# Binary cross-entropy on one core: the last full store moved to GpSimd's DMA queue, and two sets of fourteen tiny SBUF copies on SyncE

## The chip, the core and the metric

The kernel runs on one core of a Trainium2 chip. The metric is device time in microseconds of one execution; a median of several runs is given. The engines that matter are VectorE (DVE), ScalarE (ACT), GpSimd (POOL) and SyncE (SP). The first three compute or issue transfers here; SP only issues transfers. All transfers, whoever issues them, are carried out by the core's 16 DMA engines.

## The reference

```python
def setup_inputs():
    return {
        "pred": np.random.uniform(0.01, 0.99, (8192, 8192)).astype(np.float32),
        "target": np.random.randint(0, 2, (8192, 8192)).astype(np.float32),
    }

def reference(pred, target):
    eps = 1e-7
    pred = np.clip(pred, eps, 1 - eps)
    return -(target * np.log(pred) + (1 - target) * np.log(1 - pred))
```

Every element is independent. Two inputs of 256 MB each are read, one output of 256 MB is written. Targets are 0 or 1, so the loss is -log|target - 1 + pred|, and that is how the kernel computes it.

## The kernel before

The flat arrays are cut into 39 chunks, each seen as 128 partitions by some width. Chunk 0 has 8192 columns, chunks 1 to 35 have 14336 each (`WIDE`), and three tail chunks have 6656, 6656 and 1024 (`TAIL`). The index of the last wide chunk, 35, is called `z`; the tail chunks are called `a`, `b` and `c`. Prediction chunks live in a ring of three slots (`ring_p`, fp32); chunk z has the third slot, and a, b, c share the first. Target chunks live in one slot (`ring_t`), which the load converts to bf16; a, b and c take disjoint columns of it.

For each chunk there are six steps. `load_p` and `load_t` (lines 70 and 73) bring the data in. `clip` (DVE, line 85) clips the prediction in place. `merge` computes target - 1 + pred on DVE (line 91), then the absolute value and the logarithm on ACT (lines 94 and 95). `negate` (DVE, line 99) changes the sign. `store` (line 79) writes the result out. Wide chunks are computed in two halves of their columns, tail chunks in one piece.

The schedule is written by hand: each engine does its instructions in the order in which the program names them. Loads go through GpSimd's queue, apart from the first, which ACT issues. Stores go through GpSimd's queue too, up to chunk z - 1; the stores of z, a, b and c go through SP's. The last store, of chunk c, is split by rows into 108, 12 and 8 (`ROWS`).

In the loop over chunks k, the program merges k, loads the target of k + 1, negates k, clips k + 1, stores k and loads the prediction of k + 2. After the loop, chunk z is merged, and the six loads of a, b and c are issued on GpSimd. Then the order on DVE is: negate the first half of z, clip a, negate the second half of z, merge a, clip b, merge b, negate a, clip c, merge c, negate b, negate c; each store is issued by its queue when the chunk's negate is done.

Of the kernel before, what the change touches and what calls it, by code (L numbers as in the profile page):

```python
# [1 line left out]

# [4 lines left out]

EPS = 1e-7

WIDE = 14336  # L10
SLOTS = 3
TAIL = (6656, 6656, 1024)
ROWS = (108, 12, 8)


@with_exitstack
def kernel(
    ctx: ExitStack,
    tc: tile.TileContext,
    pred: bass.AP,  # L20
    target: bass.AP,
    out: bass.AP,
):
    nc = tc.nc
    fp32 = mybir.dt.float32
    low = mybir.dt.bfloat16
    Alu = mybir.AluOpType
    Act = mybir.ActivationFunctionType
    P = nc.NUM_PARTITIONS

    R, C = pred.shape
    total = R * C // P
    rest = total - sum(TAIL)
    n = rest // WIDE
    first = rest - n * WIDE
    assert 0 < first <= WIDE and n > 4 and sum(TAIL) <= WIDE
    spots = [(first, 0)]
    spots += [(WIDE, k % SLOTS * WIDE) for k in range(1, n + 1)]
    c = (n + 1) % SLOTS * WIDE
    for w in TAIL:  # L40
        spots.append((w, c))
        c += w
    n = len(spots)
    z = n - 1 - len(TAIL)
    starts = [sum(w for w, _ in spots[:k]) * P for k in range(n)]

    pool = ctx.enter_context(tc.tile_pool(name="rings", bufs=1))
    ring_p = pool.tile([P, SLOTS * WIDE], fp32, name="ring_p", tag="ring_p")
    ring_t = pool.tile([P, WIDE], low, name="ring_t", tag="ring_t")
    warm = pool.tile([1, 8], fp32, name="warm", tag="warm")  # L50

    def chunk(ap, k):
        flat = ap.rearrange("r c -> (r c)")
        w = spots[k][0]
        return flat[starts[k] : starts[k] + w * P].rearrange("(p w) -> p w", p=P)

    def cols(ring, k, part, c):
        w = spots[k][0]
        i, m = part
        return ring[:, c + i * w // m : c + (i + 1) * w // m]  # L60

    def p_of(k, part=(0, 1)):
        return cols(ring_p, k, part, spots[k][1])

    def t_of(k, part=(0, 1)):
        return cols(ring_t, k, part, spots[k][1] % WIDE)

    def load_p(k):
        queue = nc.scalar if k == 0 else nc.gpsimd
        queue.dma_start(out=p_of(k), in_=chunk(pred, k))  # L70

    def load_t(k):
        nc.gpsimd.dma_start(out=t_of(k), in_=chunk(target, k))  # L73

    def store(k):
        queue = nc.sync if k >= z else nc.gpsimd
        r = 0
        for rows in ROWS if k == n - 1 else (P,):
            queue.dma_start(out=chunk(out, k)[r : r + rows, :], in_=p_of(k)[r : r + rows, :])  # L79
            r += rows  # L80
        assert r == P

    def clip(k, *part):
        p = p_of(k, *part)
        nc.vector.tensor_scalar(  # L85
            out=p, in0=p, scalar1=EPS, scalar2=1 - EPS, op0=Alu.max, op1=Alu.min
        )

    def merge(k, *part):
        p, t = p_of(k, *part), t_of(k, *part)  # L90
        nc.vector.scalar_tensor_tensor(  # L91
            out=p, in0=t, scalar=1.0, in1=p, op0=Alu.subtract, op1=Alu.add
        )
        nc.scalar.activation(out=p, in_=p, func=Act.Abs)  # L94
        nc.scalar.activation(out=p, in_=p, func=Act.Ln)  # L95

    def negate(k, *part):
        p = p_of(k, *part)
        nc.vector.tensor_scalar(out=p, in0=p, scalar1=-1.0, scalar2=None, op0=Alu.mult)  # L99

    halves = (0, 2), (1, 2)
    with tc.manual_schedule():
        load_p(0)
        load_t(0)
        load_p(1)
        nc.vector.memset(warm, 1.0)  # L106
        nc.scalar.activation(out=warm, in_=warm, func=Act.Ln)  # L107
        for h in halves:
            clip(0, h)
        for k in range(z):  # L110
            for h in halves:
                merge(k, h)
            load_t(k + 1)
            for h in halves:
                negate(k, h)
            for h in halves:
                clip(k + 1, h)
            store(k)
            if k + 2 <= z:
                load_p(k + 2)  # L120
        for h in halves:
            merge(z, h)
        a, b, c = range(z + 1, n)
        for j in a, b, c:
            load_p(j)
            load_t(j)
        negate(z, halves[0])
        clip(a)
        negate(z, halves[1])
        store(z)  # L130
        merge(a)
        clip(b)
        merge(b)
        negate(a)
        store(a)
        clip(c)
        merge(c)
        negate(b)
        store(b)
        negate(c)  # L140
        store(c)


# [1 line left out]
_INS = ['pred', 'target']  # L145
_OUTS = [((8192, 8192), 'float32')]


# [23 lines left out]
```

## Time and profile before

| what | value |
|---|---|
| median of 3 runs | 1882.25 us (1881.54 to 1882.39) |
| the profiled execution, its own time | 1880.78 us |
| its span, first to last instruction | 1879.0 us |
| DVE busy | 1118.3 us, 60% of the span |
| ACT busy | 901.7 us, 48% |
| POOL busy (issuing transfers) | 282.8 us, 15% |
| GpSimd's queue (q0) | 652.22 MB in 16128 packets |
| SP's queue (q1) | 14.68 MB in 592 packets |
| ACT's queue (q10) | 4.19 MB in 144 packets |

The span runs from the first to the last instruction of one execution under the profiler; it and the runs' times are close but not the same, so a sum made on the span has to be carried over to the runs. In the profile, "L79" is line 79 of the kernel, "SPq" and "POOLq" are the sequencers that issue transfers, and `out<-in` names what an instruction writes and reads. The rows of busy slices cut the span into 40 equal parts; a digit 9 means 90% busy or more. "GB/s" in these rows counts the bytes on the SBUF side, where a target element has two bytes after its conversion; the HBM line counts all four. A wait in square brackets is the time the engine stood idle just before an instruction, and what ended it.

### The profile page before, as it was taken

To read this page: it belongs to the slowest core of one execution; us is meant where nothing else is said; L and a number is where in the kernel's file an instruction comes from. 1 tells how busy PE (TensorE), PEld (TensorE's weight loads), DVE (VectorE), ACT (ScalarE), POOL (GpSimd) and SP (SyncE) were. 2 spreads that over 40 slices of the span, in tenths; PEclk is the share of its full clock that TensorE was granted. 3 is DMA by queue.
4 is the path that set the end of the run, shared out by engine and by line. 5 is a ranking of instruction groups with operands and counts; after the bars stand their busy time and mean duration, and the time that the engine had idled before them with its cause. 6 is when DMAs were issued, how large, how long until landed. Compare 5 with 4: busy or idle time off the path is not lost.

```text
span 1879.0 us, 697 instructions
## 1 busy us (share of the span) xinstructions
DVE 1118.3 (60%) x226; ACT 901.7 (48%) x152; POOL 282.8 (15%) x116
## 2 busy tenths in 40 slices
DVE  4675566565555665556656555566555666665563
ACT  3555444444455555554444444555555444444473
POOL 0121111111111110111111111111101111111100
DMA  9999999999999999999999999999999999999996
GB/s 329 338 375 372 370 352 366 355 352 352 359 359 355 355 371 376 374 373 359 359 358 358 352 353 361 358 354 364 375 374 374 369 353 363 355 354 354 359 363 239
DMA packets 16869, 671.14 MB, mean 357 GB/s; under 512 B 1888, under 2 KB 1888, under 8 KB 2272
## 3 DMA queue, kind: packets, MB, share of 16 engines
q0 software_dynamic: 16128, 652.22, 97.0%
q1 hardware_dynamic: 592, 14.68, 1.8%
q10 hardware_dynamic: 144, 4.19, 0.6%
q14 instruction: 5, 0.04, 0.0%
HBM read 536.87 MB, written 268.44 MB: 429 GB/s over the span
## 4 chain that ended last, share of the span: by engine, by line
DMA 64%; issue 28%; ACT 3%; DVE 2%; another core or an unknown queue 1%; POOL 0%; POOLq 0%; DVEq 0%; PEldq 0%
DMA ring_t<-in_target_dram 64%; ACT ring_p L95 2%; ACT ring_p L94 2%; DVE ring_p L91 2%; DVE ring_p L99 0%; POOL out_dram L79 0%; DVE ring_p L85 0%; POOL ring_p L70 0%; DVEq L167 0%; POOLq L73 0%; POOLq L79 0%; DVEq L91 0%; PEldq L167 0%
## 5 line engine op out<-in xcount | busy, mean ns | idle before, releaser
L94 ACT ACTIVATE ring_p<-ring_p 128x7168 f32<-128x7168 f32 (+3 forms) x75 | 451.6, 6021 | 959.1 <-DVE ring_p L91 959.1
L91 DVE SCALAR_TENSOR_TENSOR ring_p<-ring_t,ring_p 128x7168 f32<-128x7168 bf16 (+3 forms) x75 | 554.8, 7437 | 252.2 <-DMA ring_t<-in_target_dram 252.2
L99 DVE TENSOR_SCALAR ring_p<-ring_p 128x7168 f32<-128x7168 f32 (+3 forms) x75 | 285.0, 3802 | 475.0 <-ACT ring_p L95 475.0
L95 ACT ACTIVATE ring_p<-ring_p 128x7168 f32<-128x7168 f32 (+3 forms) x75 | 452.1, 6029 | 2.4
L85 DVE TENSOR_SCALAR ring_p<-ring_p 128x7168 f32<-128x7168 f32 (+3 forms) x75 | 281.9, 3799 | 20.3 <-DMA ring_p<-in_pred_dram 20.3
L79 POOL DMA_DIRECT2D out_dram<-ring_p x35 | 126.9, 3625 | 710.8 <-DVE ring_p L99 710.8
L73 POOL DMA_DIRECT2D ring_t<-in_target_dram x39 | 20.7, 532 | 801.1 <-DVE ring_p L91 800.3
L70 POOL DMA_DIRECT2D ring_p<-in_pred_dram x38 | 135.3, 3561 | 0.0
L107 ACT ACT_TABLE_LOAD x1 | 1.3, 1283 | 1.1 <-PEq L156 1.1
L106 DVE MEMSET warm<- 1x8 f32 x1 | 0.1, 65 | 0.8 <-PEq L156 0.8
L107 ACT ACTIVATE warm<-warm 1x8 f32<-1x8 f32 x1 | 0.2, 208 | 0.0
L156 POOL MEMSET const-float32-0.0<- 128x1 f32 x1 | 0.1, 100 | 0.2 <-issue 0.2
L156 POOL MEMSET const-bfloat16-1.0<- 128x1 bf16 x1 | 0.1, 102 | 0.0
L156 POOL MEMSET const-float32-1.0<- 128x1 f32 x1 | 0.1, 100 | 0.0
L156 POOL MEMSET const-uint8-127<- 128x1 uint8 x1 | 0.1, 99 | 0.0
## 6 DMA issues: line engine op xcount, KB each, us to landing
ring_p<-in_pred_dram POOLq DMA_DIRECT2D x35, 7168.0 KB, 44.4
out_dram<-ring_p POOLq DMA_DIRECT2D x34, 7168.0 KB, 31.0
ring_t<-in_target_dram POOLq DMA_DIRECT2D x35, 3584.0 KB, 35.2
out_dram<-ring_p SPq DMA_DIRECT2D x1, 7168.0 KB, 28.9
ring_p<-in_pred_dram POOLq DMA_DIRECT2D x2, 3328.0 KB, 34.7
out_dram<-ring_p SPq DMA_DIRECT2D x2, 3328.0 KB, 9.6
ring_p<-in_pred_dram ACTq DMA_DIRECT2D x1, 4096.0 KB, 19.6
out_dram<-ring_p POOLq DMA_DIRECT2D x1, 4096.0 KB, 21.2
```

The lines of the kernel that those rows point to most:

```text
L70: queue.dma_start(out=p_of(k), in_=chunk(pred, k))
L73: nc.gpsimd.dma_start(out=t_of(k), in_=chunk(target, k))
L79: queue.dma_start(out=chunk(out, k)[r : r + rows, :], in_=p_of(k)[r : r + rows, :])
L85: nc.vector.tensor_scalar(out=p, in0=p, scalar1=EPS, scalar2=1 - EPS, op0=Alu.max, op1=Alu.min)
L91: nc.vector.scalar_tensor_tensor(out=p, in0=t, scalar=1.0, in1=p, op0=Alu.subtract, op1=Alu.add)
L94: nc.scalar.activation(out=p, in_=p, func=Act.Abs)
L95: nc.scalar.activation(out=p, in_=p, func=Act.Ln)
L99: nc.vector.tensor_scalar(out=p, in0=p, scalar1=-1.0, scalar2=None, op0=Alu.mult)
L106: nc.vector.memset(warm, 1.0)
L107: nc.scalar.activation(out=warm, in_=warm, func=Act.Ln)
L156: nc = _bacc.Bacc("TRN2", target_bir_lowering=False, num_devices=1)
```

## The change

```diff
     warm = pool.tile([1, 8], fp32, name="warm", tag="warm")
 
+    mark = pool.tile([16, 16], fp32, name="mark", tag="mark")
+    marks = pool.tile([16, 2 * 14 * 16], fp32, name="marks", tag="marks")
+
+    def copies(src, i):
+        for j in range(14):
+            r, c = 15 - j, (14 * i + j) * 16
+            nc.sync.dma_start(out=marks[:r, c : c + 16], in_=src[:r, 0:16])
+
...
     def store(k):
-        queue = nc.sync if k >= z else nc.gpsimd
+        queue = nc.sync if k > z else nc.gpsimd
...
         load_p(1)
         nc.vector.memset(warm, 1.0)
+        nc.vector.memset(mark, 1.0)
+        copies(mark, 0)
         nc.scalar.activation(out=warm, in_=warm, func=Act.Ln)
...
         negate(z, halves[0])
         clip(a)
+        copies(p_of(z), 1)
         negate(z, halves[1])
         store(z)
```

The store of chunk z, 7168 KB, is issued by GpSimd instead of SP, behind the six loads of the tail that GpSimd has issued before. The other part is two sets of fourteen transfers, each from SBUF to SBUF, issued by SP. A transfer copies 16 fp32 values (64 bytes) from each of r partitions, with r going from 15 down to 2, into columns of a tile `marks` that nothing reads. The first set reads a new small tile that DVE fills with ones and is issued at launch. The second reads the first 16 columns of chunk z and stands in the program after the clip of chunk a; on SP it comes before the stores of a, b and c.

## The prediction

> **What bounds the kernel now.** I read the busy slices first, then a table of stretches, the timeline of the last 70 us, and last the landings of single transfers.
>
> ```profile
> DMA  9999999999999999999999999999999999999996
> GB/s 329 338 375 372 370 352 366 355 352 352 359 359 355 355 371 376 374 373 359 359 358 358 352 353 361 358 354 364 375 374 374 369 353 363 355 354 354 359 363 239
> HBM read 536.87 MB, written 268.44 MB: 429 GB/s over the span
> ```
>
> The DMA engines are full in every slice but the last. One middle chunk moves 128 x 14336 x 12 bytes = 22.02 MB of HBM traffic, and the chain of waits repeats every 50.73 us, so 434 GB/s or 27.1 GB/s for each of 16 engines; no wait is hidden there that could be removed. 805.3 MB at 434 GB/s are 1855.5 us. The span is 1879.0, so about 23 us lie outside steady flow. The table shows where (columns: stretch, length, then busy us and count of DVE, ACT and POOL, granted clock, DMA share, GB/s):
>
> ```profile
> 1777.90:1814.20 36.30, 26.62 (x6) 24.60 (x4) 2.63 (x5) 1.00 1.00 382
> 1814.20:1844.50 30.30, 11.30 (x3) 11.50 (x2) 0.00 (x0) 1.00 0.94 338
> 1844.50:1855.00 10.50, 10.47 (x4) 4.18 (x1) 0.00 (x0) 1.00 0.02 3
> 1855.00:1863.00 8.00, 1.80 (x2) 7.97 (x3) 0.00 (x0) 1.00 1.00 426
> 1863.00:1866.20 3.20, 3.20 (x2) 1.35 (x2) 0.00 (x0) 1.00 0.00 0
> 1866.20:1875.50 9.30, 0.41 (x1) 0.00 (x0) 0.00 (x0) 1.00 0.92 381
> ```
>
> The DMA engines are empty for 10.5 + 3.2 = 13.7 us near the end. The timeline says why:
>
> ```profile
> 1814.18 55.22 SPq L79 DMA_DIRECT2D out_dram<-ring_p  x6
> 1821.07 3.62 DVE L85 TENSOR_SCALAR ring_p<-ring_p 128x6656 f32<-128x6656 f32 x1
> 1826.97 5.75 ACT L95 ACTIVATE ring_p<-ring_p 128x6656 f32<-128x6656 f32 x1
> 1843.69 7.09 DVE L91 SCALAR_TENSOR_TENSOR ring_p<-ring_t,ring_p 128x6656 f32<-128x6656 bf16 x1 [19.00 <-DMA ring_t<-in_target_dram]
> 1850.70 3.62 DVE L99 TENSOR_SCALAR ring_p<-ring_p 128x6656 f32<-128x6656 f32 x1
> 1856.60 5.75 ACT L95 ACTIVATE ring_p<-ring_p 128x6656 f32<-128x6656 f32 x1
> ```
>
> DVE waits 19.00 us for the target of tail chunk b. Only then come merge(b), negate(a), and the store of a (issued 1854.3), then b's own chain and its store at 1866. Chunk a was ready for its negate at 1832.7 but stands behind merge(b) in DVE's order. The target of b is late because the full store z, issued by SP at 1814.18, shares the engines with the loads still in GpSimd's queue:
>
> ```profile
> L79 POOL DMA_DIRECT2D out_dram<-ring_p x35: 3623/3626/3628, 46.3 to 1763.7; - x35
> L79 SPq DMA_DIRECT2D out_dram<-ring_p x6: 333/379/1197, 1814.2 to 1868.2; - x6
> ```
>
> The semaphore increments in the trace (one per engine and transfer) give landings from the first engine to the last: pred a 1799.4 to 1802.7, target a 1807.3 to 1810.5, pred b 1815.2 to 1820.5, target b 1835.8 to 1843.6, target c to 1846.1, store z 1840.3 to 1843.0. Alone, one 3328 KB load takes 7.87 us (1799.4 to 1807.3, and again to 1815.2); target b took 20 us on the first engine and more on the last.
>
> **The change, part by part.**
>
> *Store z from GpSimd.* Its queue has served transfers in order of issue in every landing of this trace. So store z runs after target c instead of among the loads. On the first engine: target b 1815.2 + 7.87 = 1823.0, pred and target c (2 x 1.25, by size) 1825.5. The slowest engine lags by 3.24 us from about 700 us on: target b 1826.3, target c 1828.7. GpSimd has issued all loads by 1795 and has nothing behind this store. Its issue takes 0.53 us (pred c's row) to 3.63 us (the row above), so it is written by 1818, 7 us before the loads run dry; that cover gone, it would cost those 3.6 us.
>
> The rest by the durations before: merge(b) 1826.3 to 1833.4 (7.09); negate(a), whose Ln ends at 1832.7, to 1837.1 (3.62) and store a issued at 1837.2; clip and merge of c to 1839.0; ACT on b 1833.5 to 1845.1 (2 x 5.75); negate(b) to 1848.8, store b issued; negate(c) to 1849.5, store c issued. For the DMA engines this is no longer late: store z (7168 KB, 16.9 us, as a landing step in the middle) keeps them until 1842.4 (first) and 1845.6 (slowest); store a, 7.87 us more, until 1850.3 and 1853.5; store b, ready at 1848.8 with about 1 us to first data, until 1858.1 and 1861.4. No hole is left. Store c puts up to 11 rows on 12 engines, 11 x 0.159 us (4096-byte packets) = 1.75 us: the first engines end at 1859.9; the slowest at 1861.4 if it is not among the twelve, at 1863.1 if it is. No view numbers the engines, so I take the middle, 1862.2. The span ended 1.4 us after the last landing: 1863.6, 15.4 us less than 1879.0.
>
> *First fourteen copies.* One memset of 16 x 16 (0.07 us, as the 1 x 8 one) and fourteen SP issues at 0.38 us, 5.3 us from about 1 us; SP has nothing else until 1801, so their issue costs nothing (with no such cover, 5.3 us). The copies take up to 14 slots on the busiest engine, as one row goes to one engine: the 12-row and 8-row stores post 12 and 8 increments (and one for the others together).
>
> *Second fourteen copies.* They read columns of half 0 of chunk z, so SP waits for negate(z, half 0), which ends at 1801.9; 14 x 0.38 us end at 1807.2 if nothing holds them, and store a, behind them on SP, is due at 1837.2: 30 us of cover. No later write touches what they read.
>
> *What a copy costs an engine* no row shows at 64 bytes. From below, the 4-byte semaphore packets: 0.009 us each, two per copy, 28 copies: 0.5 us. From above, the 4096-byte packets from SP, 0.159 us: 28 x 0.159 = 4.5 us. 64 bytes are nearer to 4, so I take 0.5 us on the busiest engine, and nothing at the end, since the slowest engine sets it and most engines have 3 us to spare; if the busiest is the slowest, up to 4.5 us. They can also gain: the lag between first and last engine grew from 0.6 us (first landings) to 2.4 at 300 us and 3.2 at 700, then stood still. A starting offset that keeps it from growing would end at 1859.9 + 1.4 = 1861.3, 2.3 us below the sum. I take 0.
>
> The Trainium skill (DMA: Bandwidth & Descriptors, "Anatomy of one DMA") states a fixed cost of about 2.0 us per transfer, whatever its size, which speaks against 28 tiny copies; the trace's 3328 KB store took 9.3 us to land for 7.87 us of transfer, 1.4 us of fixed part. By the page's figure an estimate for the second set one after another is 28 us, to 1830, and the sum stays as it is.
>
> *Sum.* 1879.0 - 15.4 = 1863.6 span. The profiled execution took 1880.8 with 1.8 around the span; the runs' median is 1882.25, 1.5 above it. So 1863.6 + 1.8 + 1.5 = 1866.9 us, 0.8% faster.
>
> **Rivals.**
>
> *The offset helps* (0.15): the copies stop the lag as worked out, 1864.6. For it: the lag is made in the first 700 us and the fast engines never slow. Against: half a microsecond is little beside 3.2.
>
> *The second set holds SP* (0.08). SP issues in order; if each copy waits for the one before, the set decides once it ends after about 1844, when store z is running out: 42 us / 14 = 3.0 us each. A fixed part of 1.4 plus one row ahead in each engine (1.0 us for 26624 bytes, 2.1 for 57344) is 2.4 to 3.5. At 3.5 it ends at 1850.9, 7 us late: about 1873. Against: they write separate columns and need not wait for each other.
>
> *The copies upset the engines for good* (0.07, the slower side). [...] If the copies keep the spacing from settling, the lag goes on growing: its fastest step was 0.8 us in a period (0.78 to 1.60, third period); over 35 periods 28 us, less the 3.2 already in, is 25: 1892. It decides from (15.4 + 3.2) / 35 = 0.53 us per period. Against: the lag settled in spite of two queues (ACT and GpSimd) starting together at launch.
>
> *The queue makes no difference* (0.05). The packets of both queues run on the same engines, and if these serve store z beside the loads all the same, target b lands at 1843.6 again and the time is 1882. Against: landings within GpSimd's queue never overtook each other. The Trainium skill (same page, "Issuing engines are not separate DMA queues") says that transfers run on the same 16 engines and interleave whichever engine started them, so that the choice saves sequencer time only; read strictly it gives this rival. The trace agrees on the shared engines, but the 20 us for target b show that the queue decides who is served beside whom.
>
> **How the numbers follow.** The forecast has 0.65. Faster by over 0.2% (3.8 us, about what a measurement tells from no change): forecast, offset and held SP, 0.88. Same: 0.05. Slower: 0.07. The range goes from 1863.5 (the offset case less 1 us for the estimates) to 1873 (copies at 4.5 us on the slowest engine, 1871.4, and SP held to 3.5 us each). It leaves out the last two rivals and some of the edges, under 0.2.
>
> **What would show it.** Right: DVE's wait for target b falls from 19.0 to about 2 us; store a is issued near 1837 and b near 1849; no DMA hole over 1 us after 1800; last landing near 1862. Wrong: target b landing after 1835, store a waiting on SP behind the copies, a period above 50.8 us in the middle, or a lag over 4 us between first and last engine.

## The result, and the profile after

| kernel | median | runs | ratio to the kernel before, 95% interval |
|---|---|---|---|
| before | 1881.89 us | 4 (1881.49 to 1882.39) | |
| changed | 1867.75 us | 4 (1867.36 to 1868.35) | 0.9926 [0.9911, 0.994] |

The change made the kernel faster by 14.1 us, or 0.74%, clear of its interval. The forecast was 1866.9 us.

These are the busy slices of the changed kernel's page. The last slice, which had 6 tenths before, now has 8, and the traffic over the span rose from 429 to 432 GB/s. The other DMA slices are as they were: steady flow did not change.

```profile
DMA  9999999999999999999999999999999999999998
GB/s 332 336 374 374 364 353 353 359 361 354 355 354 359 374 374 374 370 356 354 354 354 358 358 358 358 369 374 374 373 361 354 355 356 354 354 356 356 366 365 351
HBM read 536.87 MB, written 268.44 MB: 432 GB/s over the span
```

The table of stretches of the changed kernel, cut where it was cut before (stretch, length, busy us and count of DVE, ACT and POOL, clock, DMA share, GB/s):

```profile
1814.20:1844.50 30.30, 23.73 (x7) 21.67 (x4) 0.54 (x1) 1.00 1.02 369
1844.50:1855.00 10.50, 4.23 (x2) 3.33 (x3) 0.00 (x0) 1.00 0.99 427
1855.00:1863.00 8.00, 0.00 (x0) 0.00 (x0) 0.00 (x0) 1.00 0.68 266
1863.00:1866.10 3.10, 0.00 (x0) 0.00 (x0) 0.00 (x0) 1.00 0.04 16
```

The stretch from 1844.5 to 1855, whose DMA share was 0.02, is now full at 0.99, and the second hole is gone. What is left below 1 is the end itself: from about 1860 on only lagging engines and the store of c are at work. The timeline of the changed kernel says how it came about (lines 87, 93, 99, 102, 103 and 107 are what lines 79, 85, 91, 94, 95 and 99 were before):

```profile
1802.69 16.02 SPq L58 DMA_DIRECT2D marks<-ring_p  x14
1815.23 0.54 POOL L87 DMA_DIRECT2D out_dram<-ring_p  x1 [19.50 <-DVE ring_p L107]
1827.17 7.09 DVE L99 SCALAR_TENSOR_TENSOR ring_p<-ring_t,ring_p 128x6656 f32<-128x6656 bf16 x1 [1.70 <-DMA ring_t<-in_target_dram]
1834.18 3.62 DVE L107 TENSOR_SCALAR ring_p<-ring_p 128x6656 f32<-128x6656 f32 x1
1834.30 5.75 ACT L102 ACTIVATE ring_p<-ring_p 128x6656 f32<-128x6656 f32 x1 [0.80 <-DVE ring_p L99]
1837.83 15.14 SPq L87 DMA_DIRECT2D out_dram<-ring_p  x5
1845.86 4.23 DVE L107 TENSOR_SCALAR ring_p<-ring_p 128x6656 f32<-128x6656 f32 x2 [6.20 <-ACT ring_p L103]
```

GpSimd issues store z in 0.54 us. Target b lands at 1827.1 instead of 1843.6, so the wait of DVE falls from 19.00 to 1.70 us; store a goes out at 1837.8 instead of 1854.3, store b at 1849.5 instead of 1866. All of that chain now runs under store z and then store a, which keep the DMA engines full.

The packet records of the two traces, where a packet is one row of a transfer, show what had made target b late. In the kernel before, from 1817.7 to about 1833, sixteen rows of store z (57344 bytes, 2.13 us each) alternate with sixteen rows of target b (13312 bytes, 1.00 us each), as many as there are engines. So each row of target b waited behind a row of the store. In the changed kernel the rows of target b follow one another, and the first row of store z starts at 1825.5, behind the loads.

### The profile page after: what moved, and what is told of

Its sections match the earlier page's. It is cut to its first block, busy times and chain, and to the rows that moved or that the text cites. A ratio compares the mean times of both kernels' runs of the same rounds, so it can differ in the third digit from the quotient of the medians.

```text
span 1866.1 us, 728 instructions
## 1 busy us (share of the span) xinstructions
DVE 1118.2 (60%) x227; ACT 901.7 (48%) x152; POOL 283.3 (15%) x117
## 4 chain that ended last, share of the span: by engine, by line
DMA 67%; issue 28%; DVE 2%; ACT 2%; POOL 0%; POOLq 0%; DVEq 0%; PEldq 0%
DMA ring_t<-in_target_dram 67%; DVE ring_p L99 2%; ACT ring_p L103 1%; ACT ring_p L102 1%; DVE ring_p L107 0%; POOL out_dram L87 0%; POOL ring_p L78 0%; DVEq L178 0%; POOLq L81 0%; POOLq L87 0%; DVEq L99 0%; PEldq L178 0%
```

## The experiments

Twelve experiments were run, each beside runs of the kernel before on its chip: nine kernels, two of them twice, and the changed kernel once more. My theory: the gain is the order of store z and the loads and nothing else; the copies add and take nothing. The rivals: that GpSimd's queue as such brings it; that the copies help by a starting offset between the engines; that they hold SP; that they upset the engines.

**Store z moved, no copies** (`e1_move_only`, and again beside the last runs as `e10_move_again`). Against the changed kernel:

```diff
-        nc.vector.memset(mark, 1.0)
-        copies(mark, 0)
...
-        copies(p_of(z), 1)
```

> Store z from GpSimd, no copies at all. My theory (the order of store z and the loads is everything, the copies cost and bring nothing that lasts): 1867 to 1868 us, target b landing near 1827, store a issued near 1837, no empty DMA time near the end. If the copies help by their starting offset: 1869 to 1870, and a lag between first and last engine above 4 us. If the copies cost something (two sets, 0.5 to 4.5 us): 1863.5 to 1867.

> Store z from GpSimd without copies, once more. If the copies are worth nothing: within 0.7 us of the changed kernel on this chip, intervals overlapping. If they cost on the slow engines: 0.7 us or more below it. If they help: above it.

> The changed kernel once more, beside the next three on one chip. 1867 to 1868.5 us.

| kernel | median | runs | ratio to before, 95% interval |
|---|---|---|---|
| e1_move_only | 1867.09 us | 4 (1866.79 to 1868.39) | 0.9922 [0.9909, 0.9936] |
| e10_move_again | 1866.50 us | 4 (1866.30 to 1867.76) | 0.9919 [0.9905, 0.9932] |
| e12_change_again (the changed kernel) | 1869.07 us | 5 (1868.04 to 1870.42) | 0.9931 [0.9918, 0.9943] |

The moved store alone brings the whole gain. The copies don't help: over all runs the changed kernel has a median of 1868.1 us (9 runs) and the moved store alone 1866.9 (8 runs). On the last chip, where the changed kernel came out above the 1867 to 1868.5 us expected, the two sets of runs do not overlap and are 2.6 us apart, while the ratio intervals do overlap. So the copies are worth nothing at best, and probably cost 1 to 2.6 us. How they would cost that much is open: at the price of the stream of copies below, 28 copies are 0.3 us.

**One set of copies at a time.** `e3_move_first` leaves out the second set, `e4_move_second` the first.

> Store z from GpSimd and only the launch set. My theory: within 0.5 us of the kernel without copies. If the launch set delays the whole stream (targets landed 0.8 us later at the end of the changed kernel): 0.5 to 1 us slower than without it, and the last wide target lands near 1778.6 as with both sets, not near 1777.8.

> Store z from GpSimd and only the second set. My theory: within 0.5 us of the kernel without copies; the last wide target lands near 1777.8 as before the change, if the launch set is what moved it to 1778.6. If the second set costs on the slow engines: 0.5 to 1 us slower than without it.

Measured: 1867.25 us (1866.11 to 1870.79; 0.9924 [0.9911, 0.9936]) and 1868.25 us (1867.43 to 1871.18; 0.9929 [0.9916, 0.9941]). The scatter within each is larger than the half microsecond in question, so which set costs is open. Both also refute my reading that the launch set had moved the last wide target from 1777.8 to 1778.6: without the launch set it landed at 1780.7, with it alone at 1781.1. It moves by some us from one execution to another.

**The copies alone, store z still from SP** (`e2_copies_only`).

```diff
-        queue = nc.sync if k > z else nc.gpsimd
+        queue = nc.sync if k >= z else nc.gpsimd
```

> Both sets of copies, store z still from SP. My theory: 1881.5 to 1882.5 us, as before, with DVE waiting about 19 us for target b. If the copies help on their own: 1879 to 1880.5. If they hold SP: store z is issued behind the fourteen copies; in the changed kernel they kept SP until about 1819, against 1814 for store z before, so it could start up to 5 us later, which makes target b land earlier and store z later, and could move the end by some us either way: 1878 to 1885.

Measured: 1873.41 us (1870.90 to 1875.22), ratio 0.9952 [0.9939, 0.9966]. My theory, no change, was wrong here, and the rival "held SP" was right in kind but not in size: the time lies 5 us below its range. The timeline of this kernel:

```profile
1803.18 16.25 SPq L58 DMA_DIRECT2D marks<-ring_p  x14
1820.35 41.48 SPq L87 DMA_DIRECT2D out_dram<-ring_p  x6
1836.09 7.09 DVE L99 SCALAR_TENSOR_TENSOR ring_p<-ring_t,ring_p 128x6656 f32<-128x6656 bf16 x1 [10.12 <-DMA ring_t<-in_target_dram]
```

The fourteen copies held SP until store z could only go out at 1820.35, 6 us later than before. With that, target b lands 7.6 us earlier (DVE goes on at 1836.1 instead of 1843.7), and the end comes 8 us earlier. A later store z is a faster kernel: the copies work as a delay, by accident.

**Store z from SP, but held back** (`e5_sp_late`). No copies; one tiny transfer that reads target b makes SP wait for it.

```diff
     negate(z, halves[1])
+    nc.sync.dma_start(out=gate, in_=t_of(b)[:2, 0:16])
     store(z)
...
-        queue = nc.sync if k > z else nc.gpsimd
+        queue = nc.sync if k >= z else nc.gpsimd
```

> No copies, store z from SP as before, but SP first issues one copy of two rows of target b, so that store z is issued only when target b has landed. If the order is what counts (my theory): target b lands near 1827 as with GpSimd's queue, store z starts about 2 us after the loads have run dry, so 1867 to 1870 us. If the gain comes from GpSimd's queue as such: near 1880.

Measured: 1867.61 us (1867.47 to 1869.08), ratio 0.9927 [0.9915, 0.994], the same as the changed kernel. Its timeline:

```profile
1826.81 0.70 SPq L131 DMA_DIRECT2D gate<-ring_t  x1
1826.83 7.09 DVE L92 SCALAR_TENSOR_TENSOR ring_p<-ring_t,ring_p 128x6656 f32<-128x6656 bf16 x1 [1.89 <-DMA ring_t<-in_target_dram]
1827.63 25.74 SPq L80 DMA_DIRECT2D out_dram<-ring_p  x6
```

This tells the order from the queue: the same queue as before, the same gain, once the store starts behind target b. The store leaves a hole: twelve engines landed their last load at 1825.7 to 1826.5, and the first rows of store z start on all engines only at 1828.8 to 1829.0. That cost nothing that the runs can tell: the engines that led waited 2.3 to 3.1 us, the lagging ones caught up (store z landed on all sixteen within 0.2 us), and it is the lagging ones that set the end in the other kernels.

**The second set made serial** (`e8_serial14`). Store z from GpSimd, only the second set, and all copies write the same columns, so each waits for the one before.

```diff
-            r, c = 15 - j, (14 * i + j) * 16
+            r, c = 15 - j, 0
...
-        nc.vector.memset(mark, 1.0)
-        copies(mark, 0)
```

> Store z from GpSimd, and only the second set, with all fourteen copies into the same columns, so that each waits for the one before. The first copy of the second set took 5 to 6.5 us from issue to landing beside the loads. If that holds for each (rival 'held SP'): 9 copies in 45 us until the queue empties near 1846, then about 2 us each, the set ends near 1858; store a is issued then instead of at 1838, and the end moves about 14 us: 1880 to 1883. If a copy alone takes only 2.4 to 3.5 us: the set ends before 1850 and the time is 1867 to 1873.

Measured: 1882.33 us (1879.65 to 1883.98), ratio 1.0003 [0.9994, 1.0012]: the whole gain is gone. The timeline of this kernel, and below it SP's waits (waited for: us in total, times, longest):

```profile
1802.03 54.36 SPq L58 DMA_DIRECT2D marks<-ring_p  x14
1826.48 7.09 DVE L99 SCALAR_TENSOR_TENSOR ring_p<-ring_t,ring_p 128x6656 f32<-128x6656 bf16 x1 [1.66 <-DMA ring_t<-in_target_dram]
1856.50 4.71 SPq L87 DMA_DIRECT2D out_dram<-ring_p  x5
```

```profile
SPq L58 <- DMA marks<-ring_p: 44.0, 13, 8.0
```

Target b is as early as in the changed kernel, and still the end is late, since stores a, b and c stand behind the copies until 1856.5. From the issue of one copy to the issue of the next, the first six took 41.3 us (1802.0 to 1843.4) beside GpSimd's queue, 5.1 to 8.8 us each; once that queue was empty, the last seven took 1.7 us each. The Trainium skill (DMA: Bandwidth & Descriptors, "Anatomy of one DMA") gives about 2.0 us fixed per transfer, fitted there to transfers that GpSimd issues. The 1.7 us of these SP copies on idle engines is near it; the 5.1 to 8.8 us beside a full queue is 2.5 to 4.4 times the 2.0.

**A stream of copies** (`e6_launch_x35`). The launch set 35 times over.

```diff
-        copies(mark, 0)
+        for _ in range(35):
+            copies(mark, 0)
...
-        copies(p_of(z), 1)
```

> Store z from GpSimd, the launch set 35 times over (490 transfers, about 1000 us of SP at 2 us each), no second set. The records give 11 to 24 ns for a 64-byte row and 9 to 22 ns for its increment, so the busiest engine gets 490 x (20 to 46 ns) = 10 to 22 us more. If a copy costs an engine only these records, and the busiest engines are not the lagging ones: 1874 to 1886; if they are: 1877 to 1890. If the copies upset the engines' spacing, or stall an engine for longer than the records: above 1890. If they are free: 1867 to 1868.

Measured: 1872.18 us (1871.03 to 1872.65), ratio 0.995 [0.9935, 0.9965]: 5.1 us above the moved store alone (which ran on another chip), for 490 copies, so 10 ns each at the end, about half of the lowest row sum. That is between "free" and my range. In the profiled executions the end came 3.9 us later than in `e1_move_only`: the engines that led landed the last wide target 2.1 us later (1776.8 against 1774.7), and the lag between first and last engine there was 1.7 us larger (5.8 against 4.1). That lag grew slowly in the second half of the run, from about 4 to 6 us, as it also did in the changed kernel's second profile (`e12_change_again`, from 3.8 to 5.4), and about 0.1 us a period is far from the 0.53 that the rival needed. My estimate of 1000 us for the stream was off as well: it took 1799 us, 1426 of them in waits for earlier copies to land:

```profile
0.93 1799.22 SPq L58 DMA_DIRECT2D marks<-mark  x490
```

**A larger offset at launch** (`e7_wide_launch`). Two launch sets with rows of 2048 bytes, no second set.

```diff
-            r, c = 15 - j, (14 * i + j) * 16
-            nc.sync.dma_start(out=marks[:r, c : c + 16], in_=src[:r, 0:16])
+            r, c = 15 - j, j % 3 * 512
+            nc.sync.dma_start(out=marks[:r, c : c + 512], in_=src[:r, :])
...
         copies(mark, 0)
+        copies(mark, 1)
...
-        copies(p_of(z), 1)
```

> Store z from GpSimd, and at launch two sets of fourteen copies with rows of 2048 bytes instead of 64, no second set: about 0.08 us a row by the 4096-byte packets' 0.159, so the busiest engine starts with 28 x 0.08 = 2.2 us more work than the one that has none. If a starting offset decides the lag (rival 'the offset helps'): the lag between first and last engine at 700 us and later differs clearly from the 3.2 to 6.3 us of the other runs, and the time moves by 1.5 us or more, to 1865.5 or below. My theory: the lag grows as in the others, 1867 to 1869.5 us.

Measured: 1870.63 us (1869.54 to 1871.78), ratio 0.9939 [0.9925, 0.9952]; 4.1 us slower than the moved store alone on the same chip, and slower than either theory said. The lag was 3.8 us at 204 us already and stood at 4.9 from 711 us on. An offset doesn't take the place of the lag. It adds work: a row took 84 ns in the records, so 28 of them are 2.4 us on the busiest engine. In the profiled executions the engines that led landed the last wide target 1.8 us later than in `e10_move_again` (1776.6 against 1774.8), and the lag there was 1.7 us larger (4.9 against 3.2); what made it larger was not told apart.

**The last store in one piece** (`e9_move_rows128`, and again as `e11_rows128_again`). Store z moved, no copies.

```diff
-ROWS = (108, 12, 8)
+ROWS = (128,)
```

> Store z from GpSimd, no copies, and the last store in one piece of 128 rows, 8 rows on each engine instead of up to 11 on twelve. Three lagging engines were among the twelve in the changed kernel, and they set the end. 8 instead of 10 or 11 rows at 0.16 us is 0.3 to 0.5 us less, two transfers less to issue: 1866.5 to 1867 us, against 1867.1 with the split. If the lagging engines are not among the twelve, the end gets later by up to 1.3 us.

> As the one before, with the last store in one piece of 128 rows, once more: 0.3 to 0.6 us below the kernel with the split if the engines that set the end are among the twelve, so 1866.3 to 1867; the same within 0.3 if not.

Measured: 1866.45 us (1865.62 to 1868.33; 0.992 [0.9907, 0.9934]) and 1866.84 us (1866.34 to 1868.14; 0.992 [0.9907, 0.9934]). Against the split's 1867.09 and 1866.50 that is 0.6 less and 0.3 more: no difference that these runs can tell. The best version is the moved store without the copies, with the last store split or not, 1 to 2.6 us below the changed kernel.

## Why the prediction was right, point by point

*The bound and the holes.* Right. The two holes, 13.7 us, are closed, and steady flow did not change.

*Store z behind the loads.* Right in every step, all of them 0.6 to 0.9 us later, as the last wide target landed 0.8 us later in this execution (1778.6 against 1777.8): merge(b) at 1827.2 (1826.3 in the forecast), store a at 1837.8 (1837.2), store b at 1849.5 (1848.8). The issue by GpSimd took 0.54 us, the lower bound of the two. The landings of store z reached to 1849.5, later than the 1845.6 of the sum, because store a shared the engines with it; the two together end as the sum had it, at 1854.4 (1853.5).

*The end.* The sum was too low by 2.5 us in the span (1863.6 against 1866.1). The last landing came at 1864.5 instead of 1862.2. Of these 2.3 us, 0.9 come from the lagging engines: three of them were among the twelve that take the store of c (in its largest piece their increments came 1.4 to 2.5 us behind the others), where I had taken the middle. Another 1.3 us were there when store b had landed (1862.7 against 1861.4): 0.8 from the later stream, and 0.5 that was not told apart. The span ended 1.6 us after the last landing instead of 1.4. The median came nearer, 0.85 us above the forecast, because I had added 1.5 us for the distance between the profiled execution and the runs, and here it was -0.1. That nearness is luck: two misses that cancel in part.

*The copies.* Two terms were mis-sized. The issue of a copy takes 0.72 us on SP, not the 0.38 of a large store, and later copies wait: the sets took 28.7 and 16.0 us of SP instead of 5.3. In the trace the transfers of SP and ACT count their landing on eight semaphores in turn, and a copy waits until the transfer that had its semaphore before has landed. In the launch set that was the load of prediction chunk 0, issued by ACT: the eighth copy waited 13.9 us for it (the first of the two waits of the first row of waits below; the long one lies between the sets). Waits for earlier copies were 4.2 us in the launch set and 5.6 in the second. These are the issue rows of the changed kernel (durations in ns: least, median, most; first and last start), and below them SP's waits:

```profile
L58 SPq DMA_DIRECT2D marks<-mark x14: 599/722/958, 0.9 to 29.0; - x14
L58 SPq DMA_DIRECT2D marks<-ring_p x14: 599/722/862, 1802.7 to 1818.1; - x14
L87 SPq DMA_DIRECT2D out_dram<-ring_p x5: 355/395/1186, 1837.8 to 1851.8; - x5
```

```profile
SPq L58 <- DMA ring_p<-in_pred_dram: 1746.0, 2, 1732.1
SPq L58 <- DMA marks<-ring_p: 5.6, 6, 1.3
SPq L58 <- DMA marks<-mark: 4.2, 2, 3.5
```

The 30 us of cover named for the second set held: SP was free at 1818.7, and store a was due at 1837.8. And the value "nothing at the end" was probably 1 to 2.6 us too low, as the runs without copies show; the upper bound of 4.5 us held it.

*The rivals.* "The offset helps" fell: the kernels without copies are not slower, and a larger offset made the time longer. "Held SP" did not happen in the changed kernel, but `e8_serial14` shows that its mechanism and its place were right and its price too low: 5.1 to 8.8 us for a copy beside a full queue, not 2.4 to 3.5. Had each copy waited for the one before, the gain would have been lost. "The copies upset the engines" did not show at 28 or 490 copies. One of the prediction's signs of being wrong, a lag over 4 us, did come: 5.4 us in `e12_change_again`. But it came without copies too, 4.1 us in `e1_move_only` and 5.5 in `e9_move_rows128`, so it was no sign of the copies. "The queue makes no difference" is half true: with the order alike, `e5_sp_late` and the changed kernel agree, in line with the Trainium skill (DMA: Bandwidth & Descriptors, "Issuing engines are not separate DMA queues"), by which transfers run on the same engines whoever issues them. What made the 14 us is that one queue served its transfers in order, while two shared the engines row by row.

## What to carry to other kernels

When transfers set the time, look for stretches with an empty DMA share and ask which landing the stalled chain waits for; then see what is served beside that landing. Here the large store that nobody waited for belonged behind the last loads that somebody did wait for, either in the same queue or held back, and it then covered the chain. The tiny transfers cost the engines little, but they cost their issuing queue 0.7 us each and their full landing time wherever one waited for another, so nothing that matters should stand behind such copies.

## What the runs showed of the hardware that was not expected

The lag between the first and the last DMA engine grew in every run from under 1 us at the first landings to 3.0 to 6.3 us at the last wide target. In some it stood still from about 700 us (3.2 us in the kernel before); in others it went on growing to 1200 us (6.3 in `e3_move_first`) or to the end (5.4 in `e12_change_again`). The leading engines meanwhile kept a chunk in 50.7 us, 27.1 GB/s each. The lag differed between executions of one program (3.7 and 5.4 us for the changed kernel; 4.1 and 3.2 for the moved store alone). Part of the scatter between runs seems to go with it: the moved store with a lag of 3.2 us took 1866.3 us, the kernel with 6.3 took 1870.8, though one with 5.8 took 1867.8. What makes the lag was not tried.

A hole of 2.3 to 3.1 us on the leading engines removed a lag of 3.5 us (`e5_sp_late`) and did not change the time.
